# A pitch of 4128 instead of 4096 bytes for 24 blocks of split weights

## The chip, the cores and the metric

The kernel runs on one core of one Trainium2 chip. The metric is device time in microseconds (us) for one execution; a smaller number is better. All arithmetic is on the chip, in one launch.

## The reference

The reference is a trunk of two layers over 256 tokens of 1024 channels, in float32. A layer first projects its input x with one wide matrix (1024 x 10768) to the inputs of three token mixers and three merge gates:

```
proj = x @ w_in
(gq, gk, gv, gr, ga, rq, rk, rv, rg, dq, dk, dv, gate) = jnp.split(proj, IN_SPLITS, axis=-1)
y_a = o_a @ w_branch[0]      # gated linear attention, 4 heads
y_b = o_b @ w_branch[1]      # retention, 4 heads
y_c = o_c @ w_branch[2]      # windowed attention, 3 dilations x 4 heads
merged = gates[:, :, 0] * y_a + gates[:, :, 1] * y_b + gates[:, :, 2] * y_c
h = merged @ w_out
x = layer_norm(ALPHA * x + h)
x = layer_norm(ALPHA * x + (silu(x @ w_gate) * (x @ w_up)) @ w_down)     # 2816 hidden channels
```

Most of the arithmetic is in these products of 256 tokens with matrices of weights, each of which is used once in a layer.

## The kernel before, in words

**Weights.** All weights of both layers come from DRAM in the order of use as float32 units of [128, 1024] (`_stream`, line 1216). A unit lands in one of six `stage` tiles (`dma_next`, line 183). It is then split exactly into two float32r parts, a high one, which ScalarE copies with rounding (`make_hi`, line 196; now and then VectorE does it), and a low one, the rest, which VectorE subtracts (`make_lo`, line 215). float32r is the format that TensorE takes at one column per cycle. The parts lie in two of 24 blocks r0 to r23 of [128, 1024] (`R = Blocks(sb, NR, 1024, "r", F32R)`, line 168). A block is handed out first in, first out by `get` and `main` and given back by `put`. The layer's input is split in the same way into `xh` and `xl`, [128, 8, 256], with the channels on the partitions. Some other split operands also live in the blocks r: the branches' outputs (`head_out`), the merged mixer output, and the hidden activations of SwiGLU.

**Products.** One product of exact parts takes three matmuls into the same PSUM bank: high x high, high x low, low x high. Each matmul has a load of its own, of 128 columns of the stationary operand. There are two forms. `a_pair` (line 408) has weights from r as the stationary operand and moves 256 tokens, of `xh`, `xl` or, for the branch projections, of a block r. `b_unit` (line 387) has 128 tokens stationary and moves 512 columns of weights from r; the stationary operand is `xh` or `xl` for the input projections, and a block r for the output projection and for `down` (line 1094), SwiGLU's second matrix. For two of the three dilations (`dl=2`) the stationary tokens are every second column.

**Order.** The order of all instructions is fixed in the program by a planner: `issue` and `when` keep a rough clock for each engine and for each range of columns of a tile, `tick` (line 250) lets side work (attention, norms) go on by one step after each step of the main stream, and decides when the next unit is split. The clock knows the tile's name and columns (`span`, line 69) and no addresses.

**Places in memory.** Tiles lie in SBUF in the order in which they are first made: the 24 blocks r of 4096 bytes per partition, 7 blocks f4 of 4160 bytes, 10 blocks f2 of 2048 bytes, `xh` and `xl` of 8192 bytes each, the six stage tiles, the constants (`cst`, ...), `xres`, then `gah` and `gal` (the split 16 columns of a gate's first matrix, 64 bytes per k-tile), `tri`, and small tiles, among them `junk` of 512 bytes.

**The scratch tile.** `gla_all` takes the mean square of each head of gated linear attention: ScalarE squares the head with a sum on the side (line 750), and the squares themselves, which nobody reads, go to `junk`:

```
jk = T([128, 128], "junk")
for h in range(H):
    act(jk, oh[h], AF.Square, accum_out=ss[:, h:h + 1])
```

Before that, the products for `oh[h]` have read `attz[tt]`, a block f2 of [128, 512]; it is given back after the head's last instruction. Lines 130 and 118 of the profile are those of the helpers that record every matmul and every instruction of VectorE and ScalarE.

Of the kernel before, what the change touches and what calls it, by code (L numbers as in the profile page):

```python
# [8 lines left out]
F32 = mybir.dt.float32  # L9
# [45 lines left out]
def trunk(ctx: ExitStack, tc: tile.TileContext, wst, xt_in, x_in, cst, tri, pcol, wga, wa2, lnp, out):  # L55
# [5 lines left out]
    def T(shape, tag, bufs=1, dt=F32):  # L61
        return sb.tile(shape, dt, tag=tag, name=tag, bufs=bufs)

    # ---- a rough clock in ns for each engine and tile: side work goes to the tensor engine when its operands
    # should be there, so that the products with the weights needn't wait behind it ----
    clk = {"P": 0.0, "A": 0.0, "V": 0.0, "G": 0.0, "D": 0.0}
# [7 lines left out]
    def when(log, ap, e):  # L74
        """When the last access in this log to any of the columns is over, as seen by engine e."""
        name, a, b = span(ap)
        return max([t + (e != "P" and OWN if by == e else HOP) for x, y, t, by in log.get(name, ()) if x < b and a < y], default=0.0)
# [21 lines left out]
    class Timed:  # L99
        def __init__(self, engine, key, rate, fixed):  # L100
            self.engine, self.key, self.rate, self.fixed = engine, key, rate, fixed
# [38 lines left out]
    def settle(*aps, margin=MARGIN):  # L140
        """For a side generator: go on when these tiles should be there."""
        while any(when(written, a, "P") + margin > clk["P"] for a in aps):
            yield

# [1 line left out]
    class Blocks:  # L146
        def __init__(self, pool, n, cols, tag, dt=F32):
            self.free = [pool.tile([128, cols], dt, tag=f"{tag}{i}", name=f"{tag}{i}") for i in range(n)]

        def get(self, n=1):  # L150
            """For a side generator: the next n free blocks."""
            while len(self.free) < n:
                yield
            return [self.free.pop(0) for _ in range(n)]

        def main(self, n=1):
            """For the main stream."""
            left = 3000
            while len(self.free) < n:
                tick()  # L160
                left -= 1
                assert left, "blocks"
            return [self.free.pop(0) for _ in range(n)]
# [3 lines left out]

    R = Blocks(sb, NR, 1024, "r", F32R)
    F4 = Blocks(sb, N4, 1040, "f4")
# [3 lines left out]

# [1 line left out]
    state = {"dma": 0, "made": 0, "whole": 0, "calm": False, "touched": 0, "freed": 0, "cap": NR // 2}  # L175
# [3 lines left out]
    def halves(u):  # L179
        """The first unit goes by halves, for an early start."""  # L180
        return (slice(0, 512), slice(512, 1024)) if u == 0 else (slice(0, 1024),)
# [61 lines left out]

# [1 line left out]
    side = []  # L245
# [4 lines left out]
    def tick():  # L250
        for g in list(side):
            try:
                next(g)
            except StopIteration:
                side.remove(g)
        # the next unit: its first part when the engine is free for it, the second when the first should be there
        need = state["touched"] + 2
        late = clk["P"] + (CALM if state["calm"] else BACKLOG)
        if state["whole"] < state["made"]:
            hi = parts[state["whole"]][0]  # L260
            if state["whole"] < need or max(clk["V"], when(written, hi, "V")) < late:
                make_lo()
        if state["made"] < min(total, state["touched"] + AHEAD, state["whole"] + 2) and can_make():
            u = state["made"]
            there = u in staged and when(written, staged[u], "A") < clk["P"] + READY
            if u < need or there and min(clk["A"], clk["V"] - SWITCH) < late:
                make_hi()
# [14 lines left out]

# [1 line left out]
    XH = T([128, KT, S], "xh", 1, F32R)  # L284
    XL = T([128, KT, S], "xl", 1, F32R)
    xts = [F2.main()[0] for _ in range(4)]

    # the input comes in five pieces of k-tiles: 0, 1, 2-3, 4-5, 6-7
    PIECES = ((0, 1), (1, 2), (2, 4), (4, 6), (6, 8))
# [13 lines left out]

    # products of zeros while the first loads are under way bring the tensor engine to its full clock
    zero = F2.main()[0]
# [15 lines left out]
    PC = T([128, L, 32], "pcol")  # L321
    # the turning tables fill 32 partitions of their columns; the gate's second matrix and its bias lie beside them
    WA2 = C[32:49, COLS["dilc"][0]:COLS["dils"][1]].rearrange("p (l c) -> p l c", l=L)
# [8 lines left out]
    def start_rest():  # L332
        """What the first products don't need."""
        dma(nc.scalar, C[0:32, 0:512], cst[0:32, 0:512], 32)
# [47 lines left out]

# [1 line left out]
    def tokens(v, tt, dl):  # L384
        """128 tokens: the tt-th half, or with dl = 2 those of remainder tt by 2."""
        return v[:, tt * 128:tt * 128 + 128] if dl == 1 else v.rearrange("p (i c) -> p c i", c=2)[:, tt, :]
# [11 lines left out]
    def b_group(units, lh, ll, tt, ps, dl=1, last=False):  # L398
        """ps [128 tokens, 512] from units of [2 k-tiles, 512 columns], a step for each unit."""
        n = len(units)  # L400
        for i, u in enumerate(units):
            b_unit(u, i, n, lh, ll, tt, ps, dl)
            if last:
                free(u)
            if i < n - 1:
                tick()

    def a_pair(units, rh, rl, ps):
        """ps [128 columns, 2, 256 tokens] from units of [4 k-tiles, 256 columns]."""
        n = len(units)  # L410
# [21 lines left out]

# [1 line left out]
    def ln_first(tt, c, ps, st):  # L434
# [36 lines left out]

# [1 line left out]
    def dil_rot(g, ps, dst):  # L473
        """Two heads' channels [128, 2, 256 tokens] into dst, their first 32 turned; dilated groups have even tokens first."""
        dl = 2 if g else 1
# [15 lines left out]
    def dil_group(l, g, dblk, m, den, outs):  # L491
        """Scores, softmax numerators and their products with v; outs gets [128 tokens, 512] for each tile."""
        qb, kb = dblk[g, 0], dblk[g, 1]
# [117 lines left out]

# [1 line left out]
    def gla_gates(l, E):  # L613
# [50 lines left out]
    def gla_all(l, E, pss, vb, sg):  # L664
# [64 lines left out]
        for tt in range(2):  # L729
# [14 lines left out]
            ss = T([128, H], "gss", 2)  # L744
            jk = T([128, 128], "junk")
            for h in range(H):
# [14 lines left out]

# [1 line left out]
    def ret_all(l, pss, vb, sg):  # L763
# [102 lines left out]
    def head_out(l, key, o, col):  # L866
        """A branch's [tokens, heads] transposed, times its norm's gain when col is given, and split."""
        OH, OL = OT[l, key] = yield from R.get(2)
# [22 lines left out]

# [1 line left out]
    for l in range(L):  # L893
# [3 lines left out]

        # the projections for the branches: a step by tokens has two tiles, one by channels two pairs of heads
        douts = {}
# [26 lines left out]

        # the first two have their units in turns: either tile of tokens, or piece of the first input, gives them work
        us = take(8)
# [61 lines left out]

        # merge gates and branch projections, by pairs of 128 columns
        state["cap"] = (NR - 10) // 2
# [39 lines left out]

        # output projection, then the first norm
        state["cap"] = (NR - 4) // 2
# [16 lines left out]

        # SwiGLU: the first 512 channels by tokens, the others by channels
        state["cap"] = (NR - 5) // 2
# [91 lines left out]
        for tt in range(2):  # L1145
            # of the last tile, the first half of the columns ends before the second begins
            st = T([128, 2, 6], "lnst", 2)
# [60 lines left out]
def _sums(np):  # L1208
    """Within each chunk of 64, a sixteenth of the sum up to a token and of the sum after it."""
    i = np.arange(128)  # L1210
    r, q = i[:, None], i[None, :]
    same = (r // 64) == (q // 64)
    return np.concatenate([np.where(same & (r <= q), 1 / 16, 0.0), np.where(same & (r > q), 1 / 16, 0.0)], 1).astype(np.float32)


def _stream(np, w_in, w_branch, w_out, w_gate, w_up, w_down):
    """All weights in the order of use, as units of [128, 1024]."""
    w = np.empty((L * UNITS, 128, 1024), np.float32)
# [100 lines left out]
```

## Time and profile before

| | |
|---|---|
| time, median of 3 runs | 1068.72 us |
| the 3 runs | 1068.72, 1068.91, 1066.67 us |
| profiled execution, first to last instruction | 1066.5 us |
| mean granted TensorE clock | 0.995 |
| TensorE matmuls busy | 1049.8 us (98%), 7122 matmuls |
| weight loads busy | 956.9 us (90%) |
| VectorE busy | 706.6 us (66%) |
| ScalarE busy | 491.8 us (46%) |
| DMA | 192.25 MB, mean 180 GB/s |

The profile gives the profiled execution's span; a time of its own outside of that span isn't listed, so the 3 runs stand for it: they are 0.2 to 2.4 us above the span. Matmuls overlap each other, as the next one starts while the last one drains, so the duration of one matmul (276 ns and more) is longer than the distance from its start to the next one's (113 ns and more). That distance is the price that counts; a row of the chain of waits gives it as time by count.

### The profile page before, as it was taken

To read this page: it belongs to the slowest core of one execution; us is meant where nothing else is said; L and a number is where in the kernel's file an instruction comes from. 1 tells how busy PE (TensorE), PEld (TensorE's weight loads), DVE (VectorE), ACT (ScalarE), POOL (GpSimd) and SP (SyncE) were. 2 spreads that over 40 slices of the span, in tenths; PEclk is the share of its full clock that TensorE was granted. 3 is DMA by queue.
4 is the path that set the end of the run, shared out by engine and by line. 5 is a ranking of instruction groups with operands and counts; after the bars stand their busy time and mean duration, and the time that the engine had idled before them with its cause. 6 is when DMAs were issued, how large, how long until landed. Compare 5 with 4: busy or idle time off the path is not lost.

```text
span 1066.5 us, 17475 instructions
## 1 busy us (share of the span) xinstructions
PE 1049.8 (98%) x7122; PEld 956.9 (90%) x7122; DVE 706.6 (66%) x1065; ACT 491.8 (46%) x734; POOL 17.9 (2%) x24
## 2 busy tenths in 40 slices
PE   9999999999999999999999998999999999999997
PEld 7998977799998899999889998877999988999996
DVE  6798755767658756554688777476676686556454
ACT  6475554444445444343364554553443445444330
POOL 0000000000000000000000000000000000000000
PEclk9999999999999999999999999999999999999999
DMA  8786633426656574555376355343375666655521
GB/s 325 248 267 194 197 109 111 158 80 225 190 172 223 168 287 164 194 191 200 121 268 220 124 173 183 92 136 122 118 220 185 186 209 232 223 197 167 194 94 40
DMA packets 55667, 192.25 MB, mean 180 GB/s; under 512 B 6258, under 2 KB 7410, under 8 KB 55587
## 3 DMA queue, kind: packets, MB, share of 16 engines
q1 hardware_dynamic: 50400, 180.38, 51.4%
q10 hardware_dynamic: 5186, 10.76, 3.0%
q8 instruction: 56, 0.92, 0.3%
q14 instruction: 25, 0.20, 0.1%
HBM read 187.93 MB, written 3.18 MB: 179 GB/s over the span
## 4 chain that ended last, share of the span: by engine, by line
PE 90%; DVE 4%; DMA 3%; ACT 1%; issue 1%; SPq 0%; ACTq 0%; DVEq 0%
PE pm L130 70%; PE px L130 18%; DVE f L118 2%; PE px L134 2%; DMA scr<-f 2%; DVE r L118 2%; ACT f L118 1%; DMA stage<-in_wst_dram 0%; DMA f<-scr 0%; ACT r L118 0%; DVE xres L118 0%; SPq L138 0%; ACTq L138 0%; DVE lnst L118 0%; DVEq L1314 0%
## 5 line engine op out<-in xcount | busy, mean ns | idle before, releaser
L130 PE MATMUL pm<-xh,r 128*128 128x256 f32 x2688 | 478.2, 280 | 0.0
L118 DVE SCALAR_TENSOR_TENSOR r<-stage,r 128x1024 fp32r<-128x1024 f32 (+1 forms) x341 | 401.7, 1213 | 59.4 <-ACT r L118 57.1
L130 PEld LDWEIGHTS pm<-xh,r 128*128 128x128 f32 x2688 | 413.1, 189 | 1.1
L118 ACT ACTIVATE r<-stage 128x1024 fp32r<-128x1024 f32 (+1 forms) x328 | 332.8, 1051 | 91.8 <-issue 31.3
L130 PE MATMUL pm<-xl,r 128*128 128x256 f32 x1344 | 374.9, 279 | 0.0
L130 PEld LDWEIGHTS pm<-xl,r 128*128 128x128 f32 x1344 | 252.4, 188 | 0.9
L130 PE MATMUL pm<-r,xh 128*128 128x512 f32 x672 | 218.4, 406 | 0.8 <-ACT r L118 0.8
L130 PEld LDWEIGHTS pm<-r,xh 128*128 128x128 f32 x672 | 124.8, 192 | 29.3 <-issue 3.0
L130 PE MATMUL pm<-r,xl 128*128 128x512 f32 x336 | 133.6, 398 | 0.0
L118 ACT ACTIVATE f<-pm 128x512 f32<-128x512 f32 x72 | 50.8, 707 | 156.6 <-PE pm L130 106.1
L130 PE MATMUL px<-r,r 128*128 128x512 f32 x528 | 122.6, 389 | 0.0
L130 PEld LDWEIGHTS px<-r,r 128*128 128x128 f32 x528 | 97.9, 188 | 19.3
L130 PE MATMUL pm<-r,r 128*128 128x256 f32 (+1 forms) x768 | 115.1, 310 | 0.0
L130 PEld LDWEIGHTS pm<-r,r 128*128 128x128 f32 x768 | 105.2, 191 | 7.3
L118 DVE SCALAR_TENSOR_TENSOR f<-f,pm 128x512 f32<-128x512 f32 x52 | 35.6, 685 | 106.6 <-ACT f L118 89.9
L130 PEld LDWEIGHTS pm<-r,xl 128*128 128x128 f32 x336 | 64.6, 192 | 14.3
L130 PE MATMUL px<-f,f 128*128 128x128 f32 (+4 forms) x368 | 60.4, 304 | 6.3 <-DVE f L118 6.3
L130 PEld LDWEIGHTS px<-f,f 128*128 128x128 f32 (+2 forms) x368 | 48.7, 185 | 16.7 <-issue 8.5
L118 ACT ACTIVATE r<-f 128x512 fp32r<-128x512 f32 x28 | 17.7, 632 | 98.9 <-DVE f L118 98.9
L118 ACT ACTIVATE f<-pm,hcol 128x256 f32<-128x256 f32 x48 | 20.1, 471 | 58.1 <-PE pm L130 58.1
L118 ACT ACTIVATE f<-px 128x512 f32<-128x512 f32 (+2 forms) x52 | 25.0, 507 | 42.6 <-PE px L130 29.4
L118 DVE TENSOR_TENSOR f<-f,pm 128x512 f32<-128x512 f32 x22 | 15.1, 687 | 41.0 <-PE pm L130 40.8
(102 smaller groups left out, 498.6 us busy)
## 6 DMA issues: line engine op xcount, KB each, us to landing
stage<-in_wst_dram SPq DMA_DIRECT2D x339, 512.0 KB, 4.5
f<-in_lnp_dram ACTq DMA_DIRECT2D x8, 512.0 KB, 6.3
scr<-f ACTq DMA_DIRECT2D x8, 260.0 KB, 4.8
f<-scr ACTq DMA_DIRECT2D x4, 520.0 KB, 3.6
xres<-in_x_dram ACTq DMA_DIRECT2D x4, 256.0 KB, 4.0
out_dram<-xres SPq DMA_DIRECT2D x4, 256.0 KB, 2.0
f<-in_xt_dram SPq DMA_DIRECT2D x3, 256.0 KB, 9.1
cst<-in_cst_dram ACTq DMA_DIRECT2D x4, 192.0 KB, 3.8
```

The costliest lines, as they stand in the source:

```text
L118: return f(*a, **k)
L130: return nc.tensor.matmul(out, lhsT, rhs, **k)
L134: return nc.tensor.transpose(out, in_, ident)
```

## The change

The class of blocks gets a further argument, by which a tile is made wider than what is handed out of it; it is 8 columns (32 bytes) for r and none for the others. So the blocks r begin 4128 bytes apart. What is handed out is a view of the first 1024 columns. The tile `junk` is gone: the squares go to the first 128 columns of `attz[tt]`. Comments are dropped in many places, which changes no instruction.

```
-        def __init__(self, pool, n, cols, tag, dt=F32):
-            self.free = [pool.tile([128, cols], dt, tag=f"{tag}{i}", name=f"{tag}{i}") for i in range(n)]
+        def __init__(self, pool, n, cols, tag, dt=F32, gap=0):
+            self.free = [pool.tile([128, cols + gap], dt, tag=f"{tag}{i}", name=f"{tag}{i}")[:, 0:cols] for i in range(n)]
...
-    R = Blocks(sb, NR, 1024, "r", F32R)
+    R = Blocks(sb, NR, 1024, "r", F32R, 8)
...
-            jk = T([128, 128], "junk")
+            jk = attz[tt][:, 0:128]
```

## Rows read from the trace of the kernel before

**Rows 1.** The page's first part: busy us (share of the span) xinstructions.

```profile
span 1066.5 us, 17475 instructions
PE 1049.8 (98%) x7122; PEld 956.9 (90%) x7122; DVE 706.6 (66%) x1065; ACT 491.8 (46%) x734; POOL 17.9 (2%) x24
```

**Rows 2.** Waits of PE: engine line <- releaser: us in total, times, longest us.

```profile
PE px L130 <- DVE f L118: 7.7, 4, 3.2
PE px L134 <- DVE f L118: 0.8, 2, 0.5
PE pm L130 <- ACT r L118: 0.8, 1, 0.8
```

**Rows 3.** Chain of waits: start us, us, what xcount; the first three in asked stretches.

```profile
53.83 4.67 PE pm L130 x20
...
275.99 14.51 PE pm L130 x128
...
293.89 5.16 PE pm L130 x43
...
342.43 10.98 PE pm L130 x48
...
393.50 11.31 PE pm L130 x96
404.80 5.44 PE px L130 x24
```

**Rows 4.** Instructions that touch tile r: engine op xcount: ns min/median/max.

```profile
L130 PE MATMUL pm<-xh,r x2688: 276/281/469, 30.5 to 1042.4; 128*128 128x256 f32 x192
L130 PE MATMUL pm<-xl,r x1344: 276/281/286, 30.6 to 1042.3; 128*128 128x256 f32 x192
L118 DVE SCALAR_TENSOR_TENSOR r<-stage,r x341: 692/1218/1227, 4.5 to 1038.3; 128x1024 fp32r<-128x1024 f32 x170, 128x512 fp32r<-128x512 f32 x1
L118 ACT ACTIVATE r<-stage x328: 629/1052/1092, 3.9 to 1033.7; 128x1024 fp32r<-128x1024 f32 x163, 128x512 fp32r<-128x512 f32 x1
```

**Rows 5.** Groups in three stages of layer 0: xcount | busy us, mean ns.

```profile
L130 PE MATMUL pm<-xh,r 128*128 128x256 f32 x384 | 68.8, 280 | 0.0
L130 PE MATMUL pm<-xl,r 128*128 128x256 f32 x192 | 53.5, 279 | 0.0
...
L130 PE MATMUL pm<-xh,r 128*128 128x256 f32 x384 | 67.3, 278 | 0.0
L130 PE MATMUL pm<-xl,r 128*128 128x256 f32 x192 | 53.2, 277 | 0.0
...
L130 PE MATMUL pm<-xh,r 128*128 128x256 f32 x576 | 102.9, 281 | 0.0
L130 PE MATMUL pm<-xl,r 128*128 128x256 f32 x288 | 80.8, 280 | 0.0
```

**Rows 6.** Groups over the whole span: products with both operands in r, and others.

```profile
L130 PE MATMUL pm<-r,xh 128*128 128x512 f32 x672 | 218.4, 406 | 0.8 <-ACT r L118 0.8
L130 PE MATMUL px<-r,r 128*128 128x512 f32 x528 | 122.6, 389 | 0.0
L130 PE MATMUL pm<-r,r 128*128 128x256 f32 x576 | 70.9, 283 | 0.0
...
L130 PE MATMUL pm<-r,r 128*128 128x512 f32 x192 | 44.5, 390 | 0.0
```

**Rows 7.** PE in order of time, products with gah and gal: first, last, the one behind.

```profile
133.09 0.28 PE L130 MATMUL px<-xh,gah 128*16 128x256 f32 x1
...
135.77 0.28 PE L130 MATMUL px<-xh,gal 128*16 128x256 f32 x1
135.88 0.39 PE L130 MATMUL pm<-r,xh 128*128 128x512 f32 x1
```

**Rows 8.** Instructions that touch tile tri: ns min/median/max.

```profile
L130 PE MATMUL px<-r,tri x16: 279/282/366, 156.6 to 685.0; 128*128 128x256 f32 x16
```

**Rows 9.** Instructions that touch tile junk, and who waited for it (us, times).

```profile
L118 ACT ACTIVATE junk<-px x16: 277/277/279, 203.6 to 735.7; 128x128 f32<-128x128 f32 x16
L118 ACT ACTIVATION_READ_ACCUMULATOR junk<-px x16: 194/194/195, 203.8 to 735.9; 128x1 f32 x16
...
  DVE gss L118: 10.6, 4
  ACT junk L118: 4.2, 5
```

## The prediction

> **What bounds the kernel now.** I read the page's busy times first, then PE's waits, then the chain of waits, then the tile and group views of the matmuls. TensorE is the bound: matmuls fill 98% of a span of 1066.5 us and weight loads 90% [rows 1]. The reader is to see in the waits how little of the rest is waiting: the three rows of PE add up to 9.3 us in 7 waits [rows 2]. So a change that moves no work can only act through the distance from one matmul's start to the next one's, and the chain of waits gives that as time by count.
>
> The same form of matmul does not always take the same. A moving operand of 256 columns costs 14.51/128 = 113.4 ns in a stretch of the merge gates, 11.31/96 = 117.8 ns in SwiGLU, and 5.16/43 = 120.0 ns in a stretch of branch projections, where both operands lie in r. With 512 columns it is 5.44/24 = 226.7 ns with both operands in r, 10.98/48 = 228.8 ns with xh and xl stationary, and 4.67/20 = 233.5 ns where the stationary tokens are every second column [rows 3]. The durations say the same: 276 ns at least and 281 ns in the median for products of xh or xl with r [rows 4], 283 for r with r [rows 6]. 113.4 and 226.7 are one rate (0.443 ns per column), so I call them the floor. Of what lies above it I use: 5 ns more of duration (281 against 276) go with 4.4 ns more of distance (117.8 against 113.4), a factor of 0.88.
>
> How much lies above the floor, by stages of layer 0 (layer 1 has the same counts, with means that agree to 1 ns): 384 x 4 + 192 x 3 + 384 x 2 + 192 x 1 + 576 x 5 + 288 x 4 = 7104 ns of duration over 276 [rows 5]. Twice that by 0.88 is 12.5 us, or 3.1 ns for each of the 4032 a_pair products with xh or xl. The 576 branch products [rows 6] have 120.0 - 113.4 = 6.6 ns each, 3.8 us. Of 512 columns, the 528 + 192 = 720 products of r with r [rows 6] have nothing (389 and 390 ns in the mean, the branch of one price). The other 1056 (672 and 336 into pm, 48 into px on the way in) have 2.1 ns for some 864 and 6.8 ns for the 192 with every second column, 3.1 us. In all 19.4 us, the most that any placement could give back.
>
> **The change part by part.**
>
> Places. By the declared sizes the 24 blocks now begin at one phase modulo 512 bytes, and xh lies 7 x 4160 = 29120 bytes further plus whole multiples of 512, that is 448, or -64. So a_pair's weights stand 64 bytes above what is moved, b_unit's moved weights 64 above the stationary tokens, and r against r stands at 0. Afterwards block i stands at 32 i - 192 against xh (24 x 32 = 768 = 256 modulo 512): all 16 multiples of 32 occur, eight of them twice as often. Of two blocks in r the relation is 32 times the difference of their numbers, anything. All tiles behind r move together by 256, so among themselves nothing changes. The number of instructions, their waits and the planner's order stay: the planner sees names and columns, no addresses.
>
> Price of a product of 256 columns with changing phases. The trace does not show r at other phases, so I bound it by rows: 0 at the floor and 6.6 at the dearest [rows 3]. Two nearer rows lie between. The gate's products with gah and gal move xh and xl past weights whose place shifts by 64 bytes per k-tile, eight phases in turn: 24 of them take 135.88 - 133.09 = 2.79 us, 116.3 ns, 2.9 above the floor [rows 7]; but their loads are of 16 columns. The products with tri have full loads at one other phase, 282 ns in the median, 6 over 276, by the factor 5.3 [rows 8]. I take the middle, 4.1, for every product whose phases change, because neither row is nearer: one has the variety, the other the full load.
>
> Sum. a_pair with xh or xl: 4032 x (4.1 - 3.1) = +4.0 us. Branch projections: 576 x (4.1 - 6.6) = -1.4 us. The 720 products of r with r lose their one good phase: I give them the 2.1 ns of the plain products with xh [rows 3], between 0 and 6.8, +1.5 us. The 1056 with xh and xl are already off that phase: 0, between -3.1 us (floor) and 864 x 4.7 = +4.1 us (all as the worst row). Together +4.1 us: the profiled execution 1066.5 + 4.1 = 1070.6 us from first to last instruction. The timed median stands 2.2 us above that span, so 1068.7 + 4.1 = 1072.8 us. With both ends for every term: 1068.7 - 19.4 = 1049.3, and 4032 x 3.5 + 720 x 6.8 + 4.1 us = +23.1, 1091.8.
>
> The Trainium skill speaks against any effect. "TensorE: Matmul & The Clock Gate", Part 2, "Step-by-step: what each phase is for", says that TensorE has two independent read ports into SBUF, one for the moving operand and one for weight loads, so that loading the next weights takes nothing from the running matmul. By that rule the three durations 276, 281 and 283 for the same form should be one; the trace does not agree, though it does not prove that addresses are the cause. The sum by the rule would be 0, 1068.7 us. The same page, Part 1, "Wait — 56ns, not 53.3ns?", gives columns / 2.4 + 2.5 ns, an estimate of 109.2 ns for 256 columns; no product of split operands here is that short, so I leave the floor at 113.4.
>
> VectorE and ScalarE read and write the same blocks. VectorE's subtraction takes 692 ns for the half unit and 1218 for the whole: 526 ns for 512 columns more, and the longest is 1227; ScalarE's copy 629, 1052 and 1092 [rows 4]. There is no spread in them that phases could remove, and they are busy 66% and 46% [rows 1] while PE waits 9.3 us: 0. If they became 1% slower, PE's 9.3 us of waits would grow by some 0.1 us.
>
> The scratch tile. 16 squares of 277 ns, with 16 reads of the sum of 194 ns, keep their count. The products that read attz are ahead of the head that the square reads, so ScalarE already waits for them; the squares after one another into the same columns waited for each other in junk (4.2 us in 5 waits) and will in attz. What is behind them on ScalarE is other side work and the next unit's copy. New is that the next user of that f2 block waits for the squares; it is given back only behind VectorE's last step of the tile, which waits for them anyway (10.6 us in 4 waits) [rows 9]. 0, at most 4 x 4.2/5 = 3.4 us if each group held up PE.
>
> **The rivals.**
>
> Relief (faster). The phase of 64 is one where matmuls lock to the slow distance for long stretches, all of SwiGLU but its first pair; with a phase that changes from unit to unit the lock breaks and half of the price goes. For it: both 113.4 and 117.8 occur with the same operands, so the slow state can be left. Against it: the row with eight phases still pays 2.9. It gives 4032 x (1.55 - 3.1) + 576 x (1.55 - 6.6) = -9.2 us, 1059.5 us. It decides where the mean price of a product of 256 columns falls below 3.2 ns ((12.5 + 3.8 - 1.5) us / 4608).
>
> No effect. The distance is set by when the load starts against the running matmul, not by addresses: both states at one phase speak for it, the steady 120.0 of r with r against it. It is also what the skill's rule gives. 1068.7 us, within 0.5.
>
> The fast lock lost everywhere (slower still). If only a constant phase lets a stretch settle at the floor, all pay the 5.3 of tri, and r with r of 512 columns 4.5, the middle of 2.1 and 6.8: 4032 x 2.2 - 576 x 1.3 + 720 x 4.5 = +11.4 us, 1080.1 us.
>
> **How the numbers follow.** Forecast 0.35, relief 0.34, no effect 0.22, lock lost 0.09. 0.2% of 1068.7 is 2.1 us, about what a measurement of this kernel can tell from no change. Faster is relief, 0.35 with a little of the no-effect case; the same is no effect, less that, plus the low end of the forecast, 0.22; slower is the rest, 0.43. The forecast's own range is 1071 to 1077 us. The range for 8 in 10 reaches from 1057, 2.5 below the relief case (its deeper half to 1049 is left out), to 1083, above the lock-lost case.
>
> **What would show it.** Of the profile after: no stretch of the chain at 113.4 or at 117.8 for hundreds of matmuls, but a mean between 116 and 119 in the merge gates and in SwiGLU alike; r with r of 256 columns below 283 ns; r with r of 512 columns above 389 ns in `down`; VectorE's and ScalarE's durations unchanged; PE's waits still under 10 us; squares of the same length without a new wait of PE. The prediction is wrong if SwiGLU's a_pair products fall to 276 ns, or if the durations 276, 281 and 283 are where they were.

## The result, and the profile after

The kernel after takes 1079.65 us in the median of 4 runs (1078.29 to 1081.52); the kernel before, on the same chip, 1068.82 us (4 runs, 1066.67 to 1069.72). The ratio is 1.0104, with a 95% interval of 1.0088 to 1.012: slower by 11 us, in the forecast direction and inside the range for 8 in 10 (1057 to 1083), but above the forecast's own range (1071 to 1077) and 2.6 times the forecast step of 4.1 us. The spans say the same, 1077.5 against 1066.5 us, at a granted clock of 0.997 against 0.995.

The page's first part of the kernel after (busy us, share of the span, instructions) answers to [rows 1]:

```profile
span 1077.5 us, 17473 instructions
PE 1060.8 (98%) x7122; PEld 963.0 (89%) x7122; DVE 706.7 (66%) x1065; ACT 491.9 (46%) x734; POOL 17.9 (2%) x24
```

PE's waits in the kernel after (releaser: us in total, times, longest) answer to [rows 2]:

```profile
PE px L130 <- DVE f L118: 8.2, 4, 4.1
PE pm L130 <- ACT r L118: 0.6, 1, 0.6
PE pm L130 <- DVE r L118: 0.4, 2, 0.2
```

The matmuls are as many as before and 11.0 us longer busy; VectorE, ScalarE and GpSimd changed by 0.1 us at most. PE waits 9.2 us in 7 waits, before 9.3 in 7. So the loss lies inside the stream of matmuls. The chain of waits of the kernel after (start us, us, what, count), for the stretches of [rows 3] and one long one:

```profile
53.91 4.43 PE pm L130 x19
...
242.03 100.38 PE pm L130 x780
...
275.95 14.55 PE pm L130 x123
...
293.94 5.09 PE pm L130 x43
...
343.28 11.14 PE pm L130 x48
...
395.37 11.34 PE pm L130 x96
406.72 5.59 PE px L130 x24
```

The long one in the chain of the kernel before:

```profile
243.14 98.42 PE pm L130 x780
```

The reader is to see two things. Without any wait between them the same 780 matmuls take 1.96 us more. And no stretch stands at the floor any longer: the merge gates went from 113.4 to 14.55/123 = 118.3 ns, SwiGLU's second pair of products from 117.8 to 11.34/96 = 118.1, the branches from 120.0 to 5.09/43 = 118.4. Of 512 columns, r with r went from 226.7 to 5.59/24 = 232.9 ns, xh and xl stationary from 228.8 to 11.14/48 = 232.1, every second column from 233.5 to 4.43/19 = 233.2. It has become one price: about 5 ns above the floor for 256 columns and 5 to 7 for 512.

The tile view of r (count: ns min/median/max) of the kernel after, against [rows 4]:

```profile
L130 PE MATMUL pm<-xh,r x2688: 274/281/469, 29.7 to 1053.1; 128*128 128x256 f32 x192
...
L130 PE MATMUL pm<-xl,r x1344: 274/280/292, 29.8 to 1053.0; 128*128 128x256 f32 x192
...
L130 PE MATMUL px<-r,r x528: 387/394/479, 384.1 to 1069.7; 128*128 128x512 f32 x176
L118 DVE SCALAR_TENSOR_TENSOR r<-stage,r x341: 691/1218/1228, 4.6 to 1048.9; 128x1024 fp32r<-128x1024 f32 x170, 128x512 fp32r<-128x512 f32 x1
```

The median of the products with xh is 281 ns as before, which hides the change: before, the durations were two heaps, at 276 and at 281; now they spread from 274 to 290, around 280. VectorE's subtractions kept their duration to 1 ns.

The groups of xh and xl with r in the stages of layer 0 (times from 30 to 133, 216 to 317, 372 to 545 us) of the kernel after, against [rows 5]; columns as there:

```profile
L130 PE MATMUL pm<-xh,r 128*128 128x256 f32 x383 | 69.9, 282 | 0.0
L130 PE MATMUL pm<-xl,r 128*128 128x256 f32 x192 | 53.8, 280 | 0.0
...
L130 PE MATMUL pm<-xh,r 128*128 128x256 f32 x384 | 69.6, 282 | 0.0
L130 PE MATMUL pm<-xl,r 128*128 128x256 f32 x192 | 53.8, 280 | 0.0
...
L130 PE MATMUL pm<-xh,r 128*128 128x256 f32 x576 | 103.9, 281 | 0.0
L130 PE MATMUL pm<-xl,r 128*128 128x256 f32 x288 | 80.8, 281 | 0.0
```

The stages have become alike (280 to 282 ns); the gates, the cheapest before at 278 and 277, lost most. The groups over the whole span of the kernel after, against [rows 6]:

```profile
L130 PE MATMUL px<-r,r 128*128 128x512 f32 x528 | 125.4, 394 | 0.0
L130 PE MATMUL pm<-r,r 128*128 128x256 f32 x576 | 70.3, 282 | 0.0
L130 PE MATMUL pm<-r,r 128*128 128x512 f32 x192 | 45.3, 395 | 0.0
```

Of 512 columns r with r went up by 5 ns (389 to 394, 390 to 395), of 256 it went down by 1. The squares, now into a block f2, in the groups of ScalarE of the kernel after, against [rows 9]:

```profile
L118 ACT ACTIVATE f<-px 128x128 f32<-128x128 f32 x16 | 4.4, 278 | 13.0 <-PE px L130 6.0 <-issue 5.2 <-ACT f L118 1.6
```

**Where the 11 us are.** The trace has the start of every matmul. I take the distance to the next start, less the floor (113.3 or 226.7 ns), and leave out the products that stood more than 14 ns above it: the next one begins after a wait, or the granted clock is at half. The rest, in ns each and us in all:

| products | before | after | change, us |
|---|---|---|---|
| xh or xl with r, 256 columns, 4032 | 2.60, 10.40 | 4.83, 19.21 | +8.81 |
| r with r, 256 columns, 576 | 6.41, 3.67 | 5.22, 2.97 | -0.70 |
| r with r, 512 columns, 720 | 0.26, 0.18 | 5.34, 3.79 | +3.61 |
| r with xh or xl, 512 columns, 864 | 2.93, 2.34 | 5.26, 4.21 | +1.87 |
| the same, every second column, 192 | 6.59, 1.20 | 5.95, 1.08 | -0.12 |

With the small products with gah and tri (-0.08) that is +13.4 us; the late ones left out fell from 16.6 to 14.0 us above the floor. So 10.7 of the span's 11.0 us are found, and the stream itself lost more than the span shows. Most of the 2.6 us that came back belongs to the clock: before, 15 products of 512 columns ran at half the granted clock (1.2 GHz, 427 ns each), five at the start, ten from 140.5 to 144.0 us and from 666.2 to 669.6 us, after 3.5 us in which TensorE was busy for 1.25 and for 0.44 us; in the kernel after it was three, from 671.6 us, after 3.5 us of standing idle. That the change of pitch has a part in this is not shown.

### The profile page after: what moved, and what is told of

The parts are those of the page before. It is cut to its first block, busy times and chain, and to the rows that moved or that the text cites. A ratio compares the mean times of both kernels' runs of the same rounds, so it can differ in the third digit from the quotient of the medians.

```text
span 1077.5 us, 17473 instructions
## 1 busy us (share of the span) xinstructions
PE 1060.8 (98%) x7122; PEld 963.0 (89%) x7122; DVE 706.7 (66%) x1065; ACT 491.9 (46%) x734; POOL 17.9 (2%) x24
## 4 chain that ended last, share of the span: by engine, by line
PE 90%; DMA 4%; DVE 4%; ACT 1%; issue 1%; SPq 0%; ACTq 0%; DVEq 0%
PE pm L130 70%; PE px L130 18%; PE px L134 2%; DMA scr<-f 2%; DVE r L118 2%; DVE f L118 2%; DMA stage<-in_wst_dram 1%; ACT f L118 1%; DMA f<-scr 1%; ACT r L118 0%; SPq L138 0%; DVE xres L118 0%; ACTq L138 0%; DVE lnst L118 0%; DVEq L1314 0%
## 5 line engine op out<-in xcount | busy, mean ns | idle before, releaser
L130 PE MATMUL pm<-xh,r 128*128 128x256 f32 x2688 | 487.6, 282 | 0.0
L130 PE MATMUL px<-r,r 128*128 128x512 f32 x528 | 125.4, 394 | 0.0
L118 ACT ACTIVATE f<-px 128x512 f32<-128x512 f32 (+3 forms) x68 | 29.4, 453 | 55.5 <-PE px L130 35.9
```

The costliest lines, as they stand in the source:

```text
L118: return f(*a, **k)
L130: return nc.tensor.matmul(out, lhsT, rhs, **k)
```

## The experiments

I call the distance of the phases of weights and xh, modulo 512 bytes, their relation. Before it is 64 for every product with xh and xl, and 0 for r with r. The expectations number four theories: the cost is that the phase changes from one matmul to the next (1); the value of the relation sets the price (2); the loss comes from the dropped scratch tile or the moved tiles behind it, not from r's phases (3); what costs is a relation off a multiple of 64 bytes (4). Prices "above the floor" are taken from the starts in each run's trace, as in the table; which block a product reads follows from the program's fixed order, since the trace has no block numbers. All kernels but the last three lack `junk`, as the kernel after does.

**1. Same phases, without the scratch tile; and two constant shifts.** One line behind the unchanged blocks makes every tile behind them, xh included, move by 512, 64 or 256 bytes:

```
     R = Blocks(sb, NR, 1024, "r", F32R)
+    T([128, 128], "pad")        # or [128, 16], or [128, 64]
...
-            jk = T([128, 128], "junk")
+            jk = attz[tt][:, 0:128]
```

> Blocks r at the old pitch of 4096; junk is gone, and an unused tile of 512 bytes behind r moves all later tiles by 512, so every relation modulo 512 is that of the kernel before. Theory 1 (it is the change of phase from one matmul to the next that costs) and theory 2 (each phase relation between moved and stationary operand has its own price, and 64 and 0 are cheap ones) both expect 1068.8 us within 2 and SwiGLU's xh products at 281 ns, r with r of 512 columns at 389 ns. Theory 3 (the missing scratch tile or the later tiles' places cost the 11 us) expects about 1079 us.

> Old pitch, junk gone, 64 bytes behind r: xh and xl now lie at r's own phase, so every product of split operands has the relation 0, and it is constant. Both theories take the price of the relation 0 from the kernel before (r with r): 283 ns for 256 columns in all stretches (+3.5 ns x 4032 = +14 us) and 389 ns for 512 columns (-3 us), in all about 1080 us. If SwiGLU's xh products stay at 276 to 281 ns, the relation alone does not set the price.

> Old pitch, junk gone, 256 bytes behind r: xh and xl lie where they lie in the changed kernel, the relation of a_pair's weights to what they multiply is 320 bytes for all of them, constant. Theory 1: stretches settle at some constant distance, between 113.4 and 120 ns, 1060 to 1074 us, and r with r of 512 columns is at 389 ns as before. Theory 2: the relation 320 costs what it costs on average in the changed kernel, about 5 ns for 256 and for 512 columns, so xh products at 281 to 282 ns in all stretches, the 1056 products with xh stationary at 393 or more, about 1079 us less the 3.6 us of r with r, 1075 us or more.

Measured: shift512 1068.79 us, ratio 1.0006 (0.9993 to 1.0019). shift64, relation 0 throughout, 1085.03 us, 1.0153 (1.0122 to 1.0183). shift256, relation 320 throughout, 1068.61 us, 1.0003 (0.9986 to 1.002). The chain of waits in SwiGLU's second pair, first of shift512, then of shift256, then of shift64 with a stretch of its merge gates:

```profile
393.56 11.31 PE pm L130 x96
404.87 5.44 PE px L130 x24
```

```profile
396.45 11.31 PE pm L130 x96
407.76 5.44 PE px L130 x24
```

```profile
283.45 6.60 PE pm L130 x55
...
395.60 11.51 PE pm L130 x96
407.11 5.47 PE px L130 x24
```

Theory 3 falls: without the scratch tile the rows are those of before, to 0.01 us. Theory 2's 1075 us or more for shift256 was missed; shift64 came 5 us above the 1080 that both theories gave. In shift64 neither the instructions nor the constancy of phases changed, only the value, and the products with xh stand at 6.60/55 = 120.0 and 11.51/96 = 119.9 ns everywhere, 6.56 above the floor; that is what r with r, at relation 0 too, pays in every kernel here where its relation is constant (6.41 to 6.65). The tile view of shift64 shows it as one heap:

```profile
L130 PE MATMUL pm<-xl,r x1344: 278/283/284, 29.3 to 1054.1; 128*128 128x256 f32 x192
```

The same 64 bytes made the products of 512 columns with xh and xl cheaper, 1.83 against 2.93 ns above the floor: what is the dearest relation tried for 256 columns is the cheapest one tried for 512, as for r with r, which has 0.3 there before. A shift by 256 changes nothing, a first sign that the phase counts modulo 256 and not 512.

**2. Eight phases, but both parts of a unit at one.** The blocks come in pairs at one phase, the next pair 64 bytes on, and a unit's two parts take a pair (`two` finds it):

```
+    t = sb.tile([128, 1024 + (16 if i % 2 else 0)], F32R, tag=f"r{i}", name=f"r{i}")[:, 0:1024]
...
-        hi, lo = parts[u] = R.free.pop(0), R.free.pop(0)
+        hi, lo = parts[u] = R.two()
```

> Blocks r in pairs: both of a pair lie at one phase modulo 512, the next pair 64 bytes further (8 phases), and the high and the low part of a unit are always taken at one phase. The total room, and so the place of all later tiles, is that of the changed kernel. So inside a unit (12 matmuls in a_pair) no phase changes, from unit to unit it does, and all eight relations occur. Theory 1: most of the loss comes back, 1068 to 1073 us, products of 256 columns with xh settle inside a unit. Theory 2: the same mean over relations as in the changed kernel, about 5 ns each, 1077 to 1080 us.

Measured: 1079.26 us, 1.0104 (1.0083 to 1.0126); theory 1 missed, theory 2 hit with its time (its mean price of about 5 ns was 3.93). Sorted by relation, the settled price of a product with xh is 6.4 ns at 0 and 256, 5.3 at 128, 5.6 at 384, and at the odd multiples of 64 (64, 192, 320, 448) it is either 0 or 4.4. The tile view:

```profile
L130 PE MATMUL pm<-xh,r x2688: 273/280/470, 29.4 to 1051.0; 128*128 128x256 f32 x192
...
L130 PE MATMUL px<-r,r x528: 387/393/482, 384.1 to 1067.6; 128*128 128x512 f32 x176
```

In the mean the products with xh stand 3.93 above the floor, and r with r of 512 columns 4.45: its one good relation is gone here too (393 ns).

**3. A constant relation of 32.** As in 1, with `T([128, 8], "pad")`.

> Old pitch, junk gone, 32 bytes behind r: the weights of a_pair lie at the relation 32 to xh and xl, constant for all 4032 products; r against r stays at 0. Half of the changed kernel's blocks are off a multiple of 64 like this. Theory 1 (a change of phase inside the triple of high, high, low is what costs): constant, so stretches settle at a floor of 113.4 or near 117.8 as at 64, 1064 to 1074 us. Theory 4 (what costs is a place off a multiple of 64 bytes from what it meets): about 5 ns for every product with xh or xl, 281 to 282 ns in all stretches, 1078 us.

Measured: 1080.22 us, 1.0102 (1.0081 to 1.0124), theory 4's case. The chain of a stretch of its merge gates:

```profile
283.95 6.63 PE pm L130 x56
```

6.63/56 = 118.4 ns, and 5.00 above the floor over all products with xh, where a relation of 64 has 2.60. The starts go round a cycle of distances between 115 and 123 ns; no stretch settles at the floor. r with xh and xl of 512 columns pays 6.45. Half of the blocks of the kernel after stand at such odd multiples of 32.

**4. Two phases, both good; parts alike or not.** A gap of 128 bytes behind the first 12 blocks puts the halves at relations 448 and 64, both odd multiples of 64. In ab32 a unit's high part comes from one half, its low part from the other; in half32, with the same places, both come from one half; ab64 is ab32 with a gap of 256 bytes.

```
+    t = sb.tile([128, 1024 + (32 if i == NR // 2 - 1 else 0)], F32R, tag=f"r{i}", name=f"r{i}")[:, 0:1024]
...
+    hi, lo = parts[u] = R.two()     # one of each half; in half32 both of one half
```

> Old pitch, junk gone; behind the first 12 blocks r there is a gap of 128 bytes. The high part of a unit always comes from the first 12, the low part from the last 12. So a_pair's high weights lie at the relation 448 to xh, the low ones at 64, both odd multiples of 64, which alone settle at 0 or 4.4 ns; the phase changes by 128 twice in every triple, the same for all units. Theory 1: about 4.8 ns for each of the 4032 products as in the changed kernel, +9 us, and r with r of 512 columns above 389 ns, +1 to +3 us, 1077 us or more. Theory 4, and theory 2 with its price by relation: the products with xh stay as before, 2.6 ns in the mean, 1069 to 1072 us.

> The places of the run with a gap of 128 bytes behind the first 12 blocks r, but both parts of a unit now come from the same half. So a_pair's weights lie at the relation 448 or 64 to xh, both odd multiples of 64, and no phase changes inside a triple; it changes by 128 from unit to unit. If the change inside the triple was the cost of that run, the products with xh go back to 2.6 ns over the floor, r with r of 512 columns pays a part (relations 0 and 128), 1068 to 1071 us. If it was the second phase as such, they stay at 4.6 ns, 1077 us.

> High parts from the first 12 blocks, low parts from the last 12, as in the run with the gap of 128, but the gap is 256 bytes. With blocks in pairs the relations 0 and 256 cost the same (6.4 ns), and moving xh by 256 changed nothing: if the phase counts modulo 256, this kernel has no change of phase at all, 1068 us, xh products at 2.6 ns, r with r of 512 columns at 389 ns. If it counts modulo 512, the triple changes twice, 1077 us as with the gap of 128.

Measured: ab32 1076.79 us, 1.0076 (1.0053 to 1.0098); half32 1066.5 us, 0.9985 (0.9973 to 0.9996); ab64 1067.88 us, 0.9993 (0.998 to 1.0007). The chain in SwiGLU's second pair, of ab32 (with a stretch of its merge gates and one of SwiGLU's first pair), then of half32, then of ab64:

```profile
282.99 6.06 PE pm L130 x51
...
379.58 5.45 PE pm L130 x48
...
396.08 11.41 PE pm L130 x96
407.49 5.55 PE px L130 x24
```

```profile
395.41 10.94 PE pm L130 x96
406.34 5.54 PE px L130 x24
411.88 11.04 PE pm L130 x96
```

```profile
396.39 11.31 PE pm L130 x96
407.69 5.44 PE px L130 x24
```

With the same two places SwiGLU's second pair costs 11.41/96 = 118.9 ns where the weights change phase inside a triple of matmuls (high, high, low), and 10.94/96 = 114.0 where they don't: over all products with xh 4.64 against 1.57 above the floor. A change by 256 (ab64) costs nothing, 2.80 against 2.60 before: the phase counts modulo 256. For ab32 theory 1's 1077 us and 4.8 ns came close, theories 2 and 4 missed; half32 came out below its 1068 to 1071 us.

Not all of 4.64 - 1.57 is the price of the change, though. In ab32 every triple changes its phase by 128, and yet 48 products of SwiGLU's first pair take 5.45/48 = 113.5 ns, at the floor, and so do 55 of its 336 pieces of 12 products (half of what a unit is used for; the median within 1 ns of the floor counts). Of the others nearly all stand at 5 to 6, in the median at 5.5. Without such a change inside the triple the pieces stand at the floor or near 4.4: at the floor are 146 of 336 before, 130 in ab64 and 222 in half32. So the change makes the dear state 1.1 ns dearer, and fewer pieces reach the floor. Whether they miss it by the change itself or by the moments at which they begin (see 5) is not shown.

Of 512 columns r with r, now at relations 0 and 128, pays 4.07 in ab32, 3.85 in half32 and 0.26 in ab64 (where 256 counts as 0). So of the 4.1 us that half32 gains with xh and xl of 256 columns, it loses 2.5 us here.

**5. Two states at one phase.** At relation 64 a stretch runs either at 113.4 or at 117.8 ns, with the same operands. Is it set by the moment at which it starts? A short product of 64 or of 160 columns, which the next one overwrites, goes ahead of each of SwiGLU's pairs but the first, in the kernel before:

```
+            if p:
+                h0 = touch(ug[0])[0]
+                nc.tensor.matmul(pg[:, 0:64], h0[:, 0:128], XH[:, 0, 0:64], start=True, stop=True)   # or 160
```

> The kernel before with 16 matmuls more: ahead of each of SwiGLU's pairs but the first of a layer, one matmul of 64 columns into the bank that the pair's first product overwrites. It computes nothing that is used. If the distance of 117.8 ns in SwiGLU is a state that a stretch falls into by how it begins (the same relation settles at 113.4 or 117.8), a different beginning can bring it to 113.4: 1536 x 4.4 ns = -6.8 us, plus 16 x 0.11 us = +1.8, 1063.8 us, xh products there at 276 ns. If it falls back into the same state: +1.8 us, 1070.5. If the state comes from the place of the operands alone, the same 1070.5.

> As the run before, with 160 columns in the added matmul, so another offset in time at the start of each pair: 1063.8 us if it reaches the fast state, 1070.5 if not. If one of the two sizes reaches it and the other does not, the state depends on the moment of the start.

Measured: kick64 1064.06 us, 0.9957 (0.9941 to 0.9974); kick160 1069.53 us, 1.0009 (0.9996 to 1.0022). The chain of kick64, then of kick160:

```profile
392.54 0.03 PE pm L1120
392.57 10.99 PE pm L130 x96
...
502.43 11.39 PE pm L130 x96
```

```profile
392.44 0.07 PE pm L1120
392.52 11.34 PE pm L130 x96
...
505.21 10.94 PE pm L130 x96
```

One product of 0.03 us turns the 96 behind it from 11.31 to 10.99 us (114.5 ns); one of 0.07 us doesn't. At the last pair it is the other way round. The two kicks differ only in their columns, so the state depends on the moment of the start, and it stays over 96 products. Nor is it chance: before, shift512 and shift256 have the same state in at least 335 of the 336 pieces.

**6. Kicks where they help.** As kick64, without the last pair, and with one kick ahead of the second and third dilations' first products:

```
+    def kick(us, ps):
+        nc.tensor.matmul(ps[:, 0:64], touch(us[0])[0][:, 0:128], XH[:, 0, 0:64], start=True, stop=True)
...
+            if 0 < p < NPAIR - 1:
+                kick(ug, pg)
```

> The kernel before with short products of 64 columns ahead of SwiGLU's second to eighth pair of a layer (not the ninth, which follows the eighth directly) and ahead of the first a_pair of the second and the third dilation. Against the run with 16 of them: the ninth pair keeps the fast state, 2 x 96 x 4.4 ns = -0.8 us, and some 570 products of the dilations' projections that stand at 117.8 may reach 113.4, -2.5 us and +0.4 for the four products: 1061 us, ratio 0.993. If the dilations don't follow, 1063.6 us, ratio 0.9955.

Measured: 1062.9 us, 0.9949 (0.9932 to 0.9967), the fastest kernel here: 0.5% under the kernel before. All of SwiGLU's products of 256 columns, the ninth pair's too, now stand at the floor; of the dilations' 570 some 130 followed, so the 1061 us were missed by 2. Its products with xh stand 0.83 ns above the floor. The tile view shows the median at the lower heap:

```profile
L130 PE MATMUL pm<-xh,r x2688: 276/276/469, 30.6 to 1035.9; 128*128 128x256 f32 x192
```

## Why the prediction was right, and too small

**The bound and the covers: right.** 10.7 of the 11.0 us lie in the distance between matmuls' starts; VectorE's and ScalarE's durations, PE's waits, the squares (278 ns against 277) and the scratch tile came out as forecast, the last shown alone by shift512. So did the signs named ahead: 118.1 and 118.3 ns in SwiGLU and the gates (116 to 119 were named), r with r of 256 columns at 282 ns (below 283), of 512 in `down` at 394 (above 389).

**The mechanism.** The prediction left open why a place should cost, and gave one price to "changing phases". The runs show two costs. One belongs to the value of the relation: of those held for a whole unit or longer, only an odd multiple of 64 lets a triple of 256 columns run at the floor (shift64, shift32, pairs16). The other, smaller than it looks, belongs to a change within a triple (ab32 against ab64: 4.64 against 2.80). A pitch of 4128 brings both: half of the blocks stand at odd multiples of 32, and a unit's two parts are mostly neighbours, 32 bytes apart. The two do not add up: with the first alone the products stand 5.00 ns above the floor (shift32), with the second alone 4.64 (ab32), with both 4.83 (after), with means of 3.5 to 5.6 over the 16 relations and no piece at the floor. How the 4.83 divide between the two is not shown.

**The term of xh and xl with r: mis-sized, +8.8 us instead of +4.0.** The price was 4.83 and not 4.1: the row of tri (5.3), with its full loads, was near, the gate's products with gah (2.9) were not. Those 48 products had 3.08 ns before and 1.75 after, with relations that the change leaves alone: the row was no measure of changing phases. If they too have a state that depends on the start, 24 of them can't sample it; that was not tested. That is 0.7 x 4032 = 2.9 us. And what they paid before was 2.60 and not 3.1: the group means of [rows 5] hold products that begin after a wait, up to 469 ns long, which I counted as price. That is 0.5 x 4032 = 2.0 us.

**The 720 of 512 columns, r with r: +3.6 instead of +1.5 us.** Direction right; the price of the lost phase was 5.34 and not 2.1. "The plain products with xh" were not plain: they stood at 64, one of the cheaper relations for 512 columns.

**The 1056 with xh and xl: +1.75 us instead of 0.** "Already off that phase" was wrong as a reason: off 0 there is still dearer and cheaper, for the plain ones 2.93 at 64 (before), 5.26 over all relations (after), 6.45 at 32 (shift32).

**Branches: -0.7 instead of -1.4 us.** They left the dearest relation, as forecast, for 5.22 and not 4.1.

**The rivals.** "The fast lock lost everywhere" (chance 0.09, 1080.1 us) is what happened, in its outcome and its time: no stretch at the floor, 4.83 and 5.22 where it had 5.3, 5.34 where it had 4.5. It was given too little although its price came from the row with full loads. Its condition, that only a constant phase lets a stretch settle, does not hold: half32 changes phase from unit to unit and settles, shift64 is constant and doesn't. "Relief" had something right too: the slow state can be left, by another moment of the start (kick64), and half32, whose phase varies between two good values, has more pieces at the floor than the kernel before, 222 against 146. With the pitch of 4128, 18 of the 24 blocks stand at multiples of 128 or at odd multiples of 32 instead. "No effect" falls with shift64. The Trainium skill ("TensorE: Matmul & The Clock Gate", Part 2, "Step-by-step: what each phase is for") says that TensorE has two independent read ports, one for the moving operand and one for the weight loads. If that were all, their places would not matter to each other, and the runs do not agree: in shift64 the same loads and matmuls, 64 bytes apart from where they were, cost 119.9 ns instead of 117.8 in SwiGLU and 120.0 instead of 113.4 in the gates. That the two reads collide is not shown by this.

**Open.** What in SBUF or in the loads makes a relation modulo 256 bytes dear is not shown, nor why 0 is the cheapest tried for 512 columns and the dearest for 256. Both were measured with float32r alone. xh and r at good relations for both forms at once was not tried. Nor was it tried whether ab32's stretches reach the floor more often with other starts.

## What to carry to other kernels

Where matmuls bound a kernel without waiting, take the distance from start to start out of the chain, stretch by stretch, before you take means of durations: two heaps a few ns apart are a state that can be won or lost. Look for a distance of the loaded against the moved operand at which a stretch can reach the floor: shift it as a constant by steps of 32 or 64 bytes and measure, instead of spreading the phases over all values. Then keep the matmuls that follow each other at good distances, and look at how stretches begin: here one short product ahead of them was worth more than any place that was tried. A sample of a state (24 products) does not price it.

## What was not expected of the hardware

- The price of a product of 256 float32r columns depends on the distance of its two operands in SBUF modulo 256 bytes: 6.4 to 6.6 ns above the floor of 113.3 at 0, 5.3 to 5.6 at 128, 5.0 at 32, and 0 or 4.4 at 64 and 192 (before, shift64, pairs16, shift32). For 512 columns of r with r it is 0.3 at 0 (before) and 5.5 at 128 (half32).
- Where this distance changes by 128 bytes between the matmuls of a triple, the dear state is 5.5 ns and not 4.4, and 55 of 336 pieces of 12 products reach the floor, against 222 with the same places and no change inside the triple (ab32, half32), which may in part be the moments of their starts; a change by 256 costs nothing (ab64).
- At 64 there are two states, 113.4 and 117.8 ns, and a pair of SwiGLU keeps the one that it starts in over its 96 products; one matmul of 64 columns ahead of it, 0.03 us, changes which (kick64), one of 160 columns does not (kick160).
